# A two-layer hybrid decoder on one core: eight more weight units split into two fp32r parts, and the splitting done in instructions of 1024 columns

## The chip, the cores and the metric

One NeuronCore of one Trainium2 chip runs the kernel; nothing else runs on the core. The metric is the time of one execution in microseconds of device time, taken from runs on the chip. Besides the runs there is one execution recorded by the hardware profiler. Its records are what every row below is read from. Engines are named as the profile names them: PE is TensorE (matrix multiply), PEld its weight loads, DVE is VectorE, ACT is ScalarE, POOL is GpSimd, SP is the engine that issues the large DMAs.

## What is computed

256 tokens of 1024 channels pass through two layers in fp32. Cut to what matters:

```python
def reference(x, ...):
    for layer in range(2):
        h = rmsnorm(x, mix_norm[layer])
        if layer == 0:                       # conformer conv (512 ch) beside attention (8 heads x 64)
            u = h @ ab_w_in                  # 1024 x 2560
            ya = silu(layernorm(conv31(u_val * sigmoid(u_gate))))
            yb = causal_attention_with_alibi(q, k, v)
            y = concat([ya, yb]) @ ab_w_out  # 1024 x 1024
        else:                                # Griffin recurrent block
            gate, xr = split(h @ c_w_in)     # 1024 x 2048
            xr = conv4(xr) + conv_b
            y = (rg_lru(xr) * gelu(gate)) @ c_w_out   # 1024 x 1024
        x = x + y
        x = x + square(relu(rmsnorm(x, mlp_norm[layer]) @ w_up[layer])) @ w_down[layer]   # 1024 x 4096 x 1024
    return rmsnorm(x, final_norm)
```

The weights are about 96 MB in all and are read once.

## The kernel before

**Units and pieces.** Activations are kept transposed, channels on the 128 partitions and 256 tokens along the free dimension. Weights arrive in *pieces* of 1 MB (two DMAs of 512 KB, issued by SP), and each piece is two *units* of 128 x 1024 numbers. A unit is either 128 columns of a projection over all 8 blocks of input channels (kind "c", function `cols`) or 128 rows of a projection with all 1024 output columns (kind "r", function `rows`).

**Three places.** `piece` gives every piece a place. A "raw" piece lies in one of five raw buffers and is multiplied as fp32. A "pair" piece is loaded straight into one of eight pairs of buffers (`wh`, `wl`) and is multiplied as fp32 too; here the two buffers just hold the two units. A "split" piece lands in a raw buffer, and each of its units is then split into a high part `wh` (the number rounded to fp32r) and a low part `wl` (the rest), which takes one of the eight pairs for one unit. A split unit is multiplied with three fp32r matmuls instead of one fp32 matmul: `wh` with the high part of the activation, `wh` with its low part, `wl` with its high part (function `mm`). For that the activation is split as well (`split_act`: a `move` for the high part, a subtraction for the low part). An fp32 matmul shows in the trace as two instructions on `bank_a<-arena,wh` or `bank_a<-arena,wl` when a "pair" unit is used.

**Splitting a unit.** `weights` does it in two halves of 512 columns: a `move`, which either ACT (line 397) or DVE (line 398) may execute, writes half of `wh`; a DVE subtraction (line 312) writes that half of `wl`. 148 units are split this way, so there are 296 moves and 296 subtractions.

**Which units are split.** All of both MLPs (`w_up`, `w_down`), the 16 units of `c_w_in`, and four of the eight units of `ab_w_out`, those fed by the attention heads. The other four units of `ab_w_out` (fed by the conformer branch, after `ln`) and all eight of `c_w_out` (fed by the recurrent block) are "pair" units, multiplied as fp32.

**Around the projections.** `ln` in layer 0 computes mean and variance over channels with matmuls against a tile of ones, scales, and applies Silu on ACT; its results are `mx[0..3]`. `out_cols` then runs the four fp32 units of `ab_w_out`, output block by output block, and `residual_chunk` adds each pair of blocks to the residual and splits it for the MLP. In layer 1, `xr_tail` does the width-4 convolution on DVE (one tensor_scalar and three scalar_tensor_tensor), `gates` the two gate matmuls, `recur_a` an Exp, a Tanh and a square `a2`, `recur_b` a Sqrt, `recur_c` the scan, and `gate_out` the Gelu and the product `mx[c]`; `out_rows` uses `mx[0..3]` with the first four units of `c_w_out`, `out_cols` uses `mx[4..7]` with the last four.

**The order of the work.** Nothing is written in the order in which it runs. Every instruction is added to a `Plan` with an estimated cost per engine and its dependencies; `schedule` runs a list scheduler forward and backward ten times, keeps the shortest result, and `emit` issues each engine's instructions in that order. Each engine executes its own queue strictly in order, so an instruction that waits holds back everything behind it on that engine. The planner takes the DMAs in program order with a rate of 360 KB per us; parts carry a lift in rank (`weights` -2, `ln` +2).

Of the kernel before, what the change touches and what calls it, by code (L numbers as in the profile page):

```python
# [11 lines left out]
P = 128  # L12
S = 256
# [315 lines left out]
def hybrid_trunk(ctx, tc, x, mix_norm, mlp_norm, w_up, w_down, ab_w_in, ab_conv_w, ab_ln_g, ab_ln_b,  # L329
# [111 lines left out]
    def dma(out, in_, size):  # L441
        return plan.add("S", [("dma_start", (out, in_), {})], [out], [in_], {"S": 0.0}, size=size)
# [3 lines left out]
    ones = tl("ones", (P, P))  # L446
# [9 lines left out]
    shared = {t.tensor.name: f"{n}{i}" for n, ts_ in (("wh", whs), ("wl", wls)) for i, t in enumerate(ts_)}  # L456
    plan.shared = {n: 0 for n in shared}

    def renew(name, form):
        return sb.tile([P, KD * P], F32R if form % 2 else F32, name=f"{shared[name]}_{form}", tag=shared[name])  # L460
# [54 lines left out]

    def piece(kind, ap, place):
        n = len(pieces)
        pieces.append((kind, ap))
        us = [len(units), len(units) + 1]
        units.extend([(n, 0), (n, 1)])  # L520
        if place == "pair":
            i = turn["pair"] % NSPL
            turn["pair"] += 1
            homes.append((whs[i], wls[i]))
        else:
            raw = raws[turn["raw"] % NRAW]
            turn["raw"] += 1
            homes.append((raw[:, :1024], raw[:, 1024:]))
        if place == "split":
            for u in us:  # L530
                pairs[u] = turn["pair"] % NSPL
                turn["pair"] += 1
        return us
# [5 lines left out]
    def rows(ap, place):  # L539
        return piece("r", ap, place)  # L540
# [4 lines left out]
    def load(n, lo=0, hi=KD):  # L545

        taken[1] = n + 1
        kind, ap = pieces[n]
        for j, home in enumerate(homes[n]):
            if home.tensor.name in shared:  # L550
                take(home, 0)
            if kind == "ri":
                dma(home.rearrange("p (k c) -> p k c", k=KD), (c_w_r, c_w_i)[j][0].rearrange("h i j -> i h j"), P * 4096)
                continue
            if kind == "gv":
                dma(home.rearrange("p (k c) -> p k c", k=KD)[:, lo:hi], ap[j][:, lo:hi], P * 512 * (hi - lo))
                continue
            h = ap.shape[1] // 2
            a, b = (j * h, j * h + h) if kind == "r" else (max(lo, j * h), min(hi, j * h + h))
            if a < b:  # L560
                dst = home.rearrange("p (a b) -> p a b", a=h)
                dma(dst[:, a - j * h:b - j * h], ap[:, a:b], P * 4096 * (b - a) // h)

    @plan.part
    def weights(u):

        while taken[0] <= u:
            v = taken[0]
            n, j = units[v]
            taken[0] += 1  # L570
            while taken[1] <= n:
                load(taken[1])
            home = homes[n]
            if pieces[n][0] == "c":
                src = [home[k // 4].rearrange("p (k c) -> p k c", k=4)[:, k % 4, j * P:(j + 1) * P] for k in range(KD)]
                half = [home[h].rearrange("p (k c) -> p k c", k=4)[:, :, j * P:(j + 1) * P] for h in range(2)]
            else:
                t = home[j].rearrange("p (k c) -> p k c", k=KD)
                src = [t[:, k] for k in range(KD)]
                half = [t[:, :4], t[:, 4:]]  # L580
            if v not in pairs:
                got[v] = src
                continue
            wh, wl = (t[pairs[v]] for t in (whs, wls))
            take(wh, 1)
            take(wl, 1)
            wh, wl = (t.rearrange("p (k c) -> p k c", k=KD).bitcast(F32R) for t in (wh, wl))
            for h in range(2):
                q = slice(4 * h, 4 * h + 4)
                move(wh[:, q], half[h])  # L590
                tt(wl[:, q], half[h], wh[:, q].bitcast(F32), OP.subtract)
            got[v] = (wh, wl)
        return got[u]
# [15 lines left out]
    for k in (4, 6, 0, 2):  # L609
        u_o[k], u_o[k + 1] = rows(wo[:, k:k + 2], "split" if k > 3 else "pair")  # L610
# [21 lines left out]
    for k in range(0, 8, 2):  # L632
        u_co += rows(wco[:, k:k + 2], "pair")
    u_up[1], u_dn[1] = mlp_units(1)

# [13 lines left out]
    memset(ones, 1.0, "V")  # L649
    memset(eps_t, EPS, "V")  # L650
# [56 lines left out]

    def split_act(src, scale, tag, bufs, engs="V"):
        t = rot(tag, bufs, (P, 2 * S), F32R)
# [8 lines left out]

    def scaled(src, scale):
        t = rot("xg", KD)  # L720
        move(t, src, scale)
        return t
# [23 lines left out]
    def x_chunk(k):  # L746
        b = bank("a")
        transposes([(b[:, t * P:(t + 1) * P], xrow[k * XP // KD][:, t, k % (KD // XP) * P:(k % (KD // XP) + 1) * P], ident) for t in range(2)])
        xs[k] = scaled(b[:, :S], par("mix", k))
# [179 lines left out]
    def ln():  # L929
# [3 lines left out]
        mms([(b[:, :S], ones, mean, True, False)])  # L933
        mms([(b[:, :S], ones, y[3], False, True)])
        act(mean, b[:, :S], AF.Copy, scale=1.0 / 512)
        sq = [ssum, rot("nsq", 2), sumb, rot("nsq", 2)]
        for c in range(4):
            tt(y[c], y[c], mean, OP.subtract)
# [8 lines left out]
        for c in range(4):  # L947
            tt(y[c], y[c], mean, OP.mult)
            act(y[c], y[c], AF.Silu, scale=par("lng", c), bias=par("lnb", c))
            mx[c] = y[c]  # L950
# [148 lines left out]
    def xr_tail(c, b):  # L1099
# [3 lines left out]
        ts(t, xp[:, 0:S], par("cw", c), par("cb", c), OP.mult, OP.add)  # L1103
# [15 lines left out]
    def recur_a(c):  # L1119
# [5 lines left out]
        tt(a2, a, a, OP.mult)  # L1125
# [19 lines left out]
    def gate_out(c):  # L1145
        act(ym[c], ym[c], AF.Gelu_apprx_tanh)
        tt(gi[c], ym[c], xc[c], OP.mult)
        mx[c] = gi[c]
# [115 lines left out]
```

## Time and profile before

| | |
|---|---|
| median of 3 runs | 568.79 us (568.79 to 569.5) |
| the profiled execution, its own time | 569.07 us |
| its span, first to last instruction | 567.3 us |
| PE busy | 558.9 us, 2985 matmul instructions |
| PEld busy | 482.2 us |
| DVE busy | 415.4 us, 962 instructions |
| ACT busy | 310.9 us, 641 instructions |
| POOL busy | 7.5 us |
| mean granted TensorE clock | 0.998 of 2.4 GHz |
| DMA | 98.71 MB, mean 174 GB/s |

The profiled execution's own time is its span and 1.8 us around it. The end of a matmul is modelled by the profiler and matmuls overlap, so the busy time of PE is read together with the start of the next matmul: the distance between starts is what a matmul costs the queue. A group's mean duration is the time of one instruction by itself; a run of n instructions on one line of the timeline shows what they take back to back.

### The profile page before, as it was taken

Reading aid. Unit: us, or ns where it says so; the run is one execution under the profiler, and the core shown is the slowest. Engines: PE = TensorE matmul, PEld = TensorE weight load, DVE = VectorE, ACT = ScalarE, POOL = GpSimd, SP = SyncE. Lnnn points to the kernel's source line nnn. Section 1 sums busy time; section 2 is a strip of 40 time slices with the busy share of each in tenths; the row PEclk is TensorE's granted clock in tenths of the full one; section 3 lists DMA queues with packets and bytes.
Section 4 is the critical chain, followed back from the end, with each engine's and each line's share of the span. In section 5 each row is a group of like instructions: output and inputs, shape, how many; then the busy total and the mean of one; then the engine's idle time right before and its main releaser. Section 6 shows DMA issues by size and latency. Waiting matters only on the chain.

```text
span 567.3 us, 8519 instructions
## 1 busy us (share of the span) xinstructions
PE 558.9 (99%) x2985; PEld 482.2 (85%) x2985; DVE 415.4 (73%) x962; ACT 310.9 (55%) x641; POOL 7.5 (1%) x31
## 2 busy tenths in 40 slices
PE   8999999999999999999999999999999999999995
PEld 7887849988888888888889999888888888888884
DVE  2899998889766765776649999869677667757722
ACT  5104134667655656565537797728555655565623
POOL 5000000000000000000000000000000000000000
PEclk9999999999999999999999999999999999999999
DMA  8991493316666566565009738945656665662001
GB/s 241 283 375 73 138 323 134 122 56 193 196 209 192 172 200 197 175 197 174 0 1 278 242 123 280 370 157 156 199 167 191 210 192 172 202 203 93 1 1 75
DMA packets 71739, 98.71 MB, mean 174 GB/s; under 512 B 3368, under 2 KB 59776, under 8 KB 71696
## 3 DMA queue, kind: packets, MB, share of 16 engines
q1 hardware_dynamic: 71408, 98.06, 55.0%
q8 instruction: 23, 0.38, 0.3%
q14 instruction: 20, 0.16, 0.1%
q0 software_dynamic: 288, 0.11, 0.1%
HBM read 97.11 MB, written 1.05 MB: 173 GB/s over the span
## 4 chain that ended last, share of the span: by engine, by line
PE 94%; DMA 3%; DVE 2%; issue 1%; SPq 0%; ACT 0%; DVEq 0%; ACTq 0%
PE bank_b L312 50%; PE bank_a L312 44%; DMA raw<-in_ab_w_out_dram 2%; DVE arena L312 1%; DMA arena<-in_x_dram 1%; DVE wl L312 0%; SPq L312 0%; ACT arena L312 0%; ACT wh L397 0%; DVE xg L398 0%; DVE x L398 0%; DVE x L312 0%; DVE xT L398 0%; ACT tiny L312 0%; DVE tiny L312 0%
## 5 line engine op out<-in xcount | busy, mean ns | idle before, releaser
L312 DVE TENSOR_TENSOR wl<-raw,wh 128x512 fp32r<-128x512 f32 x296 | 197.0, 687 | 97.5 <-PE bank_b L312 75.6
L397 ACT ACTIVATE wh<-raw 128x512 fp32r<-128x512 f32 x265 | 163.8, 629 | 114.7 <-PE bank_a L312 53.7
L312 PE MATMUL bank_b<-x,wh 128*128 128x512 f32 (+1 forms) x768 | 169.7, 356 | 0.0
L312 PE MATMUL bank_a<-wh,f 128*128 128x512 f32 x512 | 158.5, 391 | 0.0
L312 PEld LDWEIGHTS bank_b<-x,wh 128*128 128x128 f32 x768 | 136.3, 189 | 20.3
L312 PEld LDWEIGHTS bank_a<-wh,f 128*128 128x128 f32 x512 | 94.2, 188 | 18.1
L312 PE MATMUL bank_b<-x,wl 128*128 128x256 f32 x640 | 102.6, 283 | 0.0
L312 PE MATMUL bank_a<-wl,f 128*128 128x512 f32 x256 | 99.6, 389 | 0.0
L312 PEld LDWEIGHTS bank_b<-x,wl 128*128 128x128 f32 x640 | 90.2, 191 | 2.5
L312 PEld LDWEIGHTS bank_a<-wl,f 128*128 128x128 f32 x256 | 48.1, 188 | 10.2
L312 DVE SCALAR_TENSOR_TENSOR arena<-arena,wcol 128x256 f32<-128x256 f32 x120 | 50.7, 484 | 0.2
L312 ACT ACTIVATE relu<-bank_b 128x256 f32<-128x256 f32 x64 | 24.5, 383 | 32.0 <-PE bank_b L312 30.4
L312 PE MATMUL bank_b<-xg,raw 128*128 128x256 f32 x160 | 35.8, 380 | 0.0
L312 PEld LDWEIGHTS bank_b<-xg,raw 128*128 128x128 f32 x160 | 29.9, 190 | 3.9
L312 ACT ACTIVATE relu<-relu 128x256 f32<-128x256 f32 x64 | 23.7, 410 | 17.1 <-DVE relu L312 17.0
L312 DVE TENSOR_TENSOR relu<-bank_b,relu 128x256 f32<-128x256 f32 x64 | 26.6, 419 | 3.9 <-ACT relu L312 3.9
L312 ACT ACTIVATE arena<-arena 128x256 f32<-128x256 f32 (+2 forms) x39 | 18.8, 522 | 16.2 <-DVE arena L312 15.6
L312 PE MATMUL bank_a<-arena,wl 128*128 128x256 f32 x96 | 26.3, 379 | 0.0
L312 PE MATMUL bank_a<-arena,wh 128*128 128x256 f32 x96 | 26.3, 379 | 0.0
L312 DVE TENSOR_TENSOR f<-relu,f 128x256 fp32r<-128x256 f32 x64 | 25.3, 419 | 0.5 <-ACT f L397 0.5
L312 DVE SCALAR_TENSOR_TENSOR relu<-relu,rstd 128x256 f32<-128x256 f32 x64 | 24.4, 419 | 0.1
L312 DVE TENSOR_TENSOR xT<-bank_a,xT 128x256 f32<-128x256 f32 x24 | 8.9, 419 | 15.8 <-PE bank_a L312 15.8
(127 smaller groups left out, 443.6 us busy)
## 6 DMA issues: line engine op xcount, KB each, us to landing
raw<-in_w_up_dram SPq DMA_DIRECT2D x64, 512.0 KB, 4.5
raw<-in_w_down_dram SPq DMA_DIRECT2D x64, 512.0 KB, 4.3
raw<-in_c_w_in_dram SPq DMA_DIRECT2D x16, 512.0 KB, 7.0
raw<-in_ab_w_in_dram SPq DMA_DIRECT2D x8, 512.0 KB, 8.1
wh<-in_ab_w_in_dram SPq DMA_DIRECT2D x5, 512.0 KB, 9.2
wl<-in_ab_w_in_dram SPq DMA_DIRECT2D x5, 512.0 KB, 9.6
raw<-in_ab_w_out_dram SPq DMA_DIRECT2D x4, 512.0 KB, 10.5
wh<-in_c_w_out_dram SPq DMA_DIRECT2D x4, 512.0 KB, 3.4
```

The costliest lines, as they stand in the source:

```text
L312: r.append(getattr(self.engines[o.eng], method)(*map(sub, a), **{n: sub(v) for n, v in k.items()}))
L397: return e.activation(sub(out), sub(a), AF.Copy, **({"scale": scale} if ap else {}))
```

## The change

It does these things. (1) The last four units of `ab_w_out` and the first four of `c_w_out` become "split" units; `mx[0..3]` in both layers is split by `split_act` into four tiles `xg` of twice the old width (two tiles each of the old eight make one). (2) All split units but the first four of each `w_up` and the eight of `ab_w_out` are split in one `move` and one subtraction of 1024 columns instead of two each of 512. (3) Two instructions per channel block of the recurrent layer go from DVE to ACT: the first tap of the convolution (tensor_scalar to Identity with scale and bias) and the square `a2`. (4) In `ln` the mean is taken with a tile holding 1/512, so that the copy that scaled it on ACT falls away and the subtraction reads PSUM. (5) The planner multiplies the estimated size of each DMA by a factor that depends on the length of its contiguous lines.

```diff
-    def dma(out, in_, size):
+    def dma(out, in_, size, line=4096):
+
+        size *= {512: 1.24, 1024: 1.02, 2048: 0.95}.get(line, 0.9)
         return plan.add("S", [("dma_start", (out, in_), {})], [out], [in_], {"S": 0.0}, size=size)
...
+    xgs = [tl(f"xg{i}", (P, 2 * S)) for i in range(4)]
...
             home = homes[n]
             if pieces[n][0] == "c":
...
-                half = [home[h].rearrange("p (k c) -> p k c", k=4)[:, :, j * P:(j + 1) * P] for h in range(2)]
...
-            for h in range(2):
-                q = slice(4 * h, 4 * h + 4)
-                move(wh[:, q], half[h])
-                tt(wl[:, q], half[h], wh[:, q].bitcast(F32), OP.subtract)
+
+            if pieces[n][0] == "c":
+                raw = raws[rawat[n]].rearrange("p (k c) -> p k c", k=KD)[:, :, j * P:(j + 1) * P]
+            else:
+                raw = t
+            n_ = 1 if v in whole else 2
+            for h in range(n_):
+                q = slice(KD // n_ * h, KD // n_ * (h + 1))
+                move(wh[:, q], raw[:, q])
+                tt(wl[:, q], raw[:, q], wh[:, q].bitcast(F32), OP.subtract)
             got[v] = (wh, wl)
...
-    u_o[k], u_o[k + 1] = rows(wo[:, k:k + 2], "split" if k > 3 else "pair")
+    u_o[k], u_o[k + 1] = rows(wo[:, k:k + 2], "split")
...
-        u_co += rows(wco[:, k:k + 2], "pair")
+        u_co += rows(wco[:, k:k + 2], "split" if k < 4 else "pair")
     u_up[1], u_dn[1] = mlp_units(1)
+    whole.update(u_up[0][4:] + u_dn[0] + u_xr + u_gt + u_co + u_up[1][4:] + u_dn[1])
...
+    memset(ones_c, 1.0 / 512)
...
     def split_act(src, scale, tag, bufs, engs="V"):
-        t = rot(tag, bufs, (P, 2 * S), F32R)
+        if tag == "m":
+            t = xgs[next(turns)]
+            take(t, 1)
+            t = t.bitcast(F32R)
+        else:
+            t = rot(tag, bufs, (P, 2 * S), F32R)
...
         b = bank("b")
-        mms([(b[:, :S], ones, mean, True, False)])
-        mms([(b[:, :S], ones, y[3], False, True)])
-        act(mean, b[:, :S], AF.Copy, scale=1.0 / 512)
+        mms([(b[:, :S], ones_c, mean, True, False)])
+        mms([(b[:, :S], ones_c, y[3], False, True)])
...
-            tt(y[c], y[c], mean, OP.subtract)
+            tt(y[c], y[c], b[:, :S], OP.subtract)
...
             act(y[c], y[c], AF.Silu, scale=par("lng", c), bias=par("lnb", c))
-            mx[c] = y[c]
+            mx[c] = split_act(y[c], None, "m", 4)
...
-        ts(t, xp[:, 0:S], par("cw", c), par("cb", c), OP.mult, OP.add)
+        act(t, xp[:, 0:S], AF.Identity, scale=par("cw", c), bias=par("cb", c))
...
-        tt(a2, a, a, OP.mult)
+        act(a2, a, AF.Square)
...
-        mx[c] = gi[c]
+        mx[c] = split_act(gi[c], None, "m", 4) if c < 4 else gi[c]
```

## Rows read from the trace of the kernel before

**Rows 1.** The profile page, the chain of work that ended last: each engine's share of the span.

```profile
PE 94%; DMA 3%; DVE 2%; issue 1%; SPq 0%; ACT 0%; DVEq 0%; ACTq 0%
```

**Rows 2.** Waits of PE over the whole span: who was waited for, us in total, times, the longest.

```profile
PE bank_a L312 <- DVE eps L312: 1.1, 1, 1.1
PE bank_b L312 <- DVE arena L312: 0.7, 1, 0.7
PE bank_a L312 <- DMA arena<-in_x_dram: 0.4, 1, 0.4
PE bank_b L312 <- ACT arena L312: 0.2, 1, 0.2
```

**Rows 3.** Busy time of the engines by stretch (us from the span's start, the stretch's length, then busy us and number of instructions of PE, PEld, DVE, ACT, POOL, the granted clock, the DMA share, GB/s).

```profile
84.00:97.50 13.50, 13.41 (x99) 12.09 (x99) 11.96 (x54) 6.64 (x22) 0.00 (x0) 1.00 0.45 160
97.50:109.25 11.75, 11.75 (x95) 11.49 (x94) 10.62 (x28) 8.10 (x15) 0.00 (x0) 1.00 0.26 73
109.25:123.00 13.75, 13.75 (x67) 11.83 (x65) 9.69 (x26) 5.30 (x14) 0.00 (x0) 1.00 0.26 92
123.00:301.00 178.00, 178.00 (x912) 152.49 (x911) 121.80 (x254) 106.47 (x217) 0.00 (x0) 1.00 0.51 155
...
296.50:322.20 25.70, 25.49 (x190) 24.11 (x189) 23.70 (x57) 17.96 (x37) 0.00 (x0) 1.00 0.93 286
322.20:355.30 33.10, 33.10 (x260) 32.56 (x261) 31.93 (x78) 29.77 (x56) 0.00 (x0) 1.00 0.54 182
355.30:369.10 13.80, 13.80 (x66) 12.09 (x65) 11.75 (x25) 9.55 (x18) 0.00 (x0) 1.00 1.07 370
```

**Rows 4.** Timeline of PE at the start of `c_w_out`: the first four fp32 units, 16 instructions each, and the start of what follows (start us, us, engine, line, operation, tiles, shape, count).

```profile
355.32 3.62 PE L312 MATMUL bank_a<-arena,wh 128*128 128x256 f32 x16
...
365.69 3.62 PE L312 MATMUL bank_a<-arena,wl 128*128 128x256 f32 x16
369.14 0.60 PE L312 MATMUL bank_a<-arena,wh 128*128 128x256 f32 x2
```

**Rows 5.** Timeline of PE in the split units of `ab_w_out` before: the start of one group of three matmuls, and, sixteen groups later, the start of the first fp32 unit.

```profile
103.50 0.40 PE L312 MATMUL bank_a<-x,wh 128*128 128x256 f32 x2
...
109.25 0.60 PE L312 MATMUL bank_a<-arena,wh 128*128 128x256 f32 x2
```

**Rows 6.** Groups of instructions by line, engine, operation and shape: count, then busy us and mean ns of one, then the idle time before them and its releasers.

```profile
L312 DVE TENSOR_TENSOR wl<-raw,wh 128x512 fp32r<-128x512 f32 x296 | 197.0, 687 | 97.5 <-PE bank_b L312 75.6 <-ACT wh L397 18.0 <-PE bank_a L312 3.6
L397 ACT ACTIVATE wh<-raw 128x512 fp32r<-128x512 f32 x265 | 163.8, 629 | 114.7 <-PE bank_a L312 53.7 <-PE bank_b L312 36.9 <-DMA raw<-in_ab_w_out_dram 9.0
...
L312 DVE TENSOR_TENSOR f<-relu,f 128x256 fp32r<-128x256 f32 x64 | 25.3, 419 | 0.5 <-ACT f L397 0.5
...
L397 ACT ACTIVATE f<-relu 128x256 fp32r<-128x256 f32 x53 | 19.3, 402 | 0.1
L312 ACT ACT_TABLE_LOAD x15 | 19.2, 1283 | 1.8 <-PE bank_b L312 0.9 <-PEq L1250 0.7
...
L312 DVE TENSOR_SCALAR arena<-arena,pcol 128x256 f32<-128x256 f32 x8 | 3.1, 414 | 0.0
...
L312 ACT ACTIVATE arena<-arena 128x1024 f32<-128x1024 f32 x2 | 2.1, 1057 | 0.4 <-issue 0.4
L312 ACT ACTIVATE arena<-arena,pcol 128x256 f32<-128x256 f32 x4 | 2.1, 591 | 0.0
```

**Rows 7.** Timeline of ACT and of DVE just after the recurrence: eight moves and nine subtractions of 512 columns back to back.

```profile
360.02 4.25 ACT L397 ACTIVATE wh<-raw 128x512 fp32r<-128x512 f32 x8
...
361.29 5.50 DVE L312 TENSOR_TENSOR wl<-raw,wh 128x512 fp32r<-128x512 f32 x9
```

**Rows 8.** Timeline around 44 us of ACT, DVE and PE: the first splits of `ab_w_out`, and the wait of PE behind them.

```profile
44.16 0.69 DVE L312 TENSOR_TENSOR wl<-raw,wh 128x512 fp32r<-128x512 f32 x1 [1.32 <-ACT wh L397]
...
45.17 0.42 DVE L312 SCALAR_TENSOR_TENSOR arena<-bank_b,rstd 128x256 f32<-128x256 f32 x1
...
45.73 0.89 PE L312 MATMUL bank_b<-arena 64*128 64x256 f32 x4 [0.71 <-DVE arena L312]
```

**Rows 9.** Timeline of DVE and ACT at the end of `ln`: the reciprocal of the standard deviation, a subtraction of `weights` for the MLP put between, the products, the load of the Silu table, the four Silu, and later subtractions for the MLP.

```profile
104.26 1.75 DVE L312 RECIPROCAL arena<-arena 128x256 f32<-128x256 f32 x1
105.93 0.63 DVE L312 TENSOR_TENSOR wl<-raw,wh 128x512 fp32r<-128x512 f32 x1
106.48 1.42 DVE L312 TENSOR_TENSOR arena<-arena 128x256 f32<-128x256 f32 x4
107.81 1.28 DVE L312 TENSOR_TENSOR wl<-raw,wh 128x512 fp32r<-128x512 f32 x2
...
107.10 1.28 ACT L312 ACT_TABLE_LOAD   x1
108.40 2.08 ACT L312 ACTIVATE arena<-arena,pcol 128x256 f32<-128x256 f32 x4
```

**Rows 10.** Waits of ACT for the DMAs of `c_w_in` (us in total, times, the longest).

```profile
ACT wh L397 <- DMA raw<-in_c_w_in_dram: 4.5, 7, 1.1
```

**Rows 11.** Timeline of SP: the issue of the last two pieces of `ab_w_out`, of the last piece of `c_w_out`, and of the first pieces of the second `w_up`.

```profile
62.14 0.33 SPq L312 DMA_DIRECT2D wh<-in_ab_w_out_dram  x1
...
344.29 0.38 SPq L312 DMA_DIRECT2D wl<-in_c_w_out_dram  x1
...
348.81 5.30 SPq L312 DMA_DIRECT2D raw<-in_w_up_dram  x6
```

More of the change, by code (lines that the diff above doesn't have):

```diff
@@ L439, in small_dma @@
         return plan.add("G", [("dma_start", (out, in_), {})], [out], [in_], {"G": 0.55}, lag=4.0)
-    def dma(out, in_, size):
+    def dma(out, in_, size, line=4096):
+        size *= {512: 1.24, 1024: 1.02, 2048: 0.95}.get(line, 0.9)
         return plan.add("S", [("dma_start", (out, in_), {})], [out], [in_], {"S": 0.0}, size=size)
     ident = tl("ident", (P, P))
-    ones = tl("ones", (P, P))
+    ones, ones_c = tl("ones", (P, P)), tl("ones_c", (P, P))
     pcol = tl("pcol", (P, P))
@@ L455, in hybrid_trunk @@
     wls = [tl(f"wl{i}", (P, KD * P)) for i in range(NSPL)]
-    shared = {t.tensor.name: f"{n}{i}" for n, ts_ in (("wh", whs), ("wl", wls)) for i, t in enumerate(ts_)}
+    xgs = [tl(f"xg{i}", (P, 2 * S)) for i in range(4)]
+    shared = {t.tensor.name: (f"{n}{i}", list(t.shape)) for n, ts_ in (("wh", whs), ("wl", wls), ("xg", xgs))
+              for i, t in enumerate(ts_)}
     plan.shared = {n: 0 for n in shared}
     def renew(name, form):
-        return sb.tile([P, KD * P], F32R if form % 2 else F32, name=f"{shared[name]}_{form}", tag=shared[name])
+        tag, shape = shared[name]
+        return sb.tile(shape, F32R if form % 2 else F32, name=f"{tag}_{form}", tag=tag)
     def take(t, part):
@@ L514, in hybrid_trunk @@
     turn = {"raw": 0, "pair": 0}
+    rawat, whole = {}, set()
     def piece(kind, ap, place):
@@ L526, in piece @@
             raw = raws[turn["raw"] % NRAW]
+            rawat[n] = turn["raw"] % NRAW
             turn["raw"] += 1
@@ L552, in load @@
             if kind == "ri":
-                dma(home.rearrange("p (k c) -> p k c", k=KD), (c_w_r, c_w_i)[j][0].rearrange("h i j -> i h j"), P * 4096)
+                dma(home.rearrange("p (k c) -> p k c", k=KD), (c_w_r, c_w_i)[j][0].rearrange("h i j -> i h j"), P * 4096, 512)
                 continue
             if kind == "gv":
-                dma(home.rearrange("p (k c) -> p k c", k=KD)[:, lo:hi], ap[j][:, lo:hi], P * 512 * (hi - lo))
+                dma(home.rearrange("p (k c) -> p k c", k=KD)[:, lo:hi], ap[j][:, lo:hi], P * 512 * (hi - lo), 512)
                 continue
@@ L561, in load @@
                 dst = home.rearrange("p (a b) -> p a b", a=h)
-                dma(dst[:, a - j * h:b - j * h], ap[:, a:b], P * 4096 * (b - a) // h)
+                dma(dst[:, a - j * h:b - j * h], ap[:, a:b], P * 4096 * (b - a) // h, ap.shape[2] * 4)
     @plan.part
@@ L579, in weights @@
                 src = [t[:, k] for k in range(KD)]
-                half = [t[:, :4], t[:, 4:]]
             if v not in pairs:
@@ L706, in narrow @@
             mms([(b[:, :S], w[1][:, j, :], xs[j][0], False, j == KD - 1) for j in range(k, k + 4)])
+    turns = (i % len(xgs) for i in range(1000))
     def split_act(src, scale, tag, bufs, engs="V"):
-        t = rot(tag, bufs, (P, 2 * S), F32R)
+        if tag == "m":
[4 more added lines that the diff above has]
+            t = rot(tag, bufs, (P, 2 * S), F32R)
         h, lo = t[:, :S], t[:, S:]
@@ L717, in split_act @@
         return h, lo, t
[L719 to L722, printed above, removed]
     def residual_chunk(k, acc, gname, g0, xs):
@@ L748, in x_chunk @@
         transposes([(b[:, t * P:(t + 1) * P], xrow[k * XP // KD][:, t, k % (KD // XP) * P:(k % (KD // XP) + 1) * P], ident) for t in range(2)])
-        xs[k] = scaled(b[:, :S], par("mix", k))
+        xs[k] = xgs[k // 2][:, k % 2 * S:(k % 2 + 1) * S]
+        move(xs[k], b[:, :S], par("mix", k))
         move(xT[k], b[:, :S])
```

## The prediction

> **What bounds the kernel now.** I read the chain of waits first: the reader should see there that 94% of the span is PE [rows 1], so time is won mainly by asking less of PE. Then the waits of PE: inside the run it stands still for 0.7 us behind DVE and 0.2 us behind ACT, and the other two entries are the start-up [rows 2]. So there is next to no idle time of PE to win back; a change of DVE or ACT alone can win about 0.9 us. Third, the table by stretch, for the cover under PE. In the first MLP DVE is busy 121.80 of 178 us and ACT 106.47, a third of slack. In the recurrent block, 296.5 to 355.3, DVE is busy 23.70 + 31.93 = 55.63 of 58.8 us and ACT 17.96 + 29.77 = 47.73: 3.2 and 11.1 us free, 14.2 together. There PE is fed just in time [rows 3].
>
> **The eight units, on PE.** Before, four fp32 units take 369.14 - 355.32 = 13.82 us, 3.455 us each [rows 4]. Split, a unit is eight groups of three matmuls; sixteen such groups run from 103.50 to 109.25, which makes 5.75 / 2 = 2.875 us a unit [rows 5]. The gain is 0.58 us a unit, 8 x 0.58 = **4.64 us**. The split groups are of exactly this shape (256 columns, fp32r), so this size is measured, not guessed, and PE has no other work beside it that would hide it.
>
> **What the eight units cost elsewhere.** Each needs a move of `wh` and a subtraction of `wl`. The four of `ab_w_out` go in halves: on DVE 8 x 0.687 = 5.5 us by the mean of one, 8 x 0.61 = 4.9 back to back (5.50 us for nine) [rows 6, 7]; on ACT 8 x 0.53 to 0.63 = 4.2 to 5.0. Those of `c_w_out` go whole. Splitting `mx` adds a move of 0.40 and a subtraction of 0.42 us for each of eight chunks [rows 6], on a path that ends at PE.
>
> *Layer 0.* The four units and `mx[0..3]` must be ready when `out_cols` begins, at 109.25 before. Silu starts at 108.40 and four take 2.08 [rows 9], so `mx[0]` is ready within 0.3 us of its use: the path through `ln` is just in time, and the split of `mx` puts about 0.40 + 0.42 and two hand-overs, some 1.1 us, behind it. Against that, the copy of the mean on ACT goes (about 0.4 us), and the planner has 0.63 us of MLP subtraction standing between the reciprocal and the products which it can move away. DVE has to fit 4.9 to 5.5 us of `wl` and 1.7 of `mx` before about 110; it is free for 13.5 - 11.96 + 11.75 - 10.62 = 2.7 us from 84 on, and the MLP's subtractions now done there (three in rows 9, more after 109) can wait. Net I take a stall of **0.5 us**; bounds 0 (all fits into the gaps) and 2.5 (1.1 of latency, and 6.6 less 2.7 less 2.5 of work that finds no place). What was pushed back must be done by the start of the MLP: the stretch from 109.25 shrinks by 2.3 us, DVE has 13.75 - 9.69 = 4.1 free in it [rows 3]; four units in halves want 5.5, but the second pair is needed only one pass of PE later, so I add nothing and keep 1 us for the range.
>
> *Layer 1.* `out_rows` needs one unit and one `mx` each 2.9 us from about 355 on, and DVE has 2 us free in the 13.8 after that, ACT 4.2 [rows 3]. For the whole block to 355 I count pessimistically, with all four units in it. ACT: eight Identity by the row of the same form (two per-partition operands), 8 x 0.59 = 4.7; eight squares by the nearest 256-column row, 8 x 0.40 = 3.2; four moves of 1024, by the 1024-column row at most 1.06 each, 4.2; four moves of `mx`, 1.6. DVE loses 8 x 0.414 and 8 x 0.42 = 6.7 and gains four subtractions, 0.61 + 512 x (0.687 - 0.419) / 256 = 1.15 each, 4.6, and 1.7 for `mx`. With the gain of the wide instructions below, ACT +12.1 and DVE -1.6: 10.5 us more for 14.2 us of slack, of which the moves may go to either engine. It fits, barely; I take a stall of **0.5 us**, bounds 0 and 2.5 (three chunks of added hand-over of 0.8).
>
> **Wide instructions.** A move of 1024 columns bounds from above at 1.06 us (a 1024-column ACT row that also accumulates), two of 512 are 1.26 by their means [rows 6]: 0.2 us a unit. But the row of eight back to back says 4.25 / 8 = 0.53 us each [rows 7], so two cost 1.06 and one of 1024, at 0.53 + 0.43, about 0.96: 0.1 us a unit. For DVE likewise 1.22 against 1.15, 0.07 us, where the means would give 0.15. I take the back-to-back values, since the moves mostly stand in runs. For the 140 wide units it is 14 us of ACT and 10 of DVE, nearly all under PE in the MLPs: worth **0**. A wide pair hands over later: the low part is complete after 0.96 + 1.15 us instead of 0.53 + 2 x 0.61, some 0.36 us later; eight buffer pairs, two passes ahead, cover that in the MLPs. If that cover were gone (a unit split only as it is used), 0.36 us for each of 140, 50 us, is the outer end, and no row shows PE waiting for `wh` or `wl` in the MLPs, so I give it no weight.
>
> **DMAs and queues.** Eight 512 KB transfers change their buffer. The last two pieces of `ab_w_out`, issued from 62.14 on when their pairs came free, go to raw buffers which are free by about 40; they come earlier, and the pieces behind them on SP too. The first two pieces of `c_w_out` go to raw buffers; the last two wait for later projections, so the `w_up` pieces behind them on SP (first at 348.81 [rows 11]) slip by some 3 us, and are used only past 380: nothing. POOL gets one more memset at the start, nothing waits for it.
>
> **The planner's rates.** ACT and then DVE wait for the first `ab_w_out` piece at 44 us because the plan had it there earlier; DVE loses 1.32 us and PE 0.71 [rows 8]. With lines of 512 bytes counted 1.24 times, the plan expects it later. Of the 0.7 us I take **0.3**; bounds -0.7 and +0.7, as the new order may put another wait there.
>
> **The sum.** 569.07 (the profiled execution: a span of 567.3 and 1.8 around it) - 4.64 + 0.5 + 0.5 - 0.3 = 565.1. The median of the runs is 0.28 lower than that execution, so **564.8 us**.
>
> **Rivals.**
>
> *Late hand-overs.* The two stalls lie nearer their upper ends, 1 to 2 us each and the 0.7 us at 44 stays: 569.07 - 4.64 + 2 to 4 - 0.28, 566.2 to 568.2, 567 in the middle. For it: Silu starting at 108.40 for a use at 109.25, and DVE at 32 of 33 us. Against: the small steps of DVE around 88 to 98 belong to layer 1 and can wait.
>
> *ACT becomes the bound in the recurrent block.* If the planner leaves the moves on ACT, 12.1 us more meet 11.1 us of slack, of which 4.5 us is waiting for DMAs of `c_w_in` [rows 10] in strict order, with Identity, which the convolution now needs, queued behind it; and a changed order can add table loads at 1.28 us [rows 6]. The block then ends 12.1 - 11.1 + 4.5 + 2 x 1.28 = 8.1 us later: 569.07 - 4.64 + 8.1 - 0.28 = 572.3, slower. It decides once the block's lateness passes 4.6 us. Against: DVE has 1.6 us less to do in the block than before, so the planner has somewhere to put moves. The rows show a first tap at 0.414 us on DVE and at 0.59 on ACT, a square at about 0.42 and 0.40 [rows 6]. The Trainium skill, page "ScalarE: Activation LUTs", section "Rules for kernel authors", says that multiplies and adds belong on VectorE and not on ScalarE, which speaks against part (3) of the change. By that rule the block would lose the eight differences of the taps if all of them lay on the path, 8 x 0.18 = 1.4 us, and the sum would be 566.2; the trace of before bears the rule out for the tap, not for the square.
>
> *The change doesn't free PE.* If the order shifts elsewhere by as much as the units give (a start of the MLP held up, a wait at the start), the time stays: 568.5. Only the fitting planner could do it; no row names the place.
>
> *More than the sum.* No stall, and the whole 0.9 us of waits gone: 569.07 - 4.64 - 0.9 - 0.28 = 563.2; lower it can hardly go, since PE's work then has no gap left but start and end.
>
> **Chances.** Forecast (563.4 to 566.3) 0.60; late hand-overs (566.3 to 568.2) 0.20; ACT the bound 0.12; no gain 0.04; more than the sum 0.04. The range 563.2 to 568.3 leaves out the ACT case, part of the last two, under 0.2. What a measurement tells from no change is about 0.2%, 1.1 us, so faster is below 567.65: 0.60 + 0.04 + 0.16 of the late hand-overs = 0.80. Within 0.2%: 0.04 of these, 0.04 of no gain and 0.01 of the ACT case, 0.09. Slower: 0.11.
>
> **What would show it.** The fp32 matmuls on `bank_a<-arena,wh` and `,wl` should fall from 96 each to 32, and new fp32r groups of `bank_a` with `xg` start every 0.36 us; moves and subtractions of 1024 should count 140 and take about 1.06 and 1.22 us alone, those of 512 32. The time from the first `ab_w_out` unit to the MLP should fall by 2.3 us and the `c_w_out` stretch too. It would be wrong if PE showed waits of over 1 us for ACT or DVE around 109 or between 310 and 367, if ACT shows more than 15 table loads, or if the MLP passes of PE became longer.

## The result and the profile after

The changed kernel takes 565.69 us (median of 4 runs, 565.48 to 566.32), the kernel before 569.1 beside it (568.79 to 569.5). The ratio is 0.9944, 95% interval 0.9928 to 0.9959: 3.4 us faster, where 4.0 were forecast. The profiled execution took 565.66 us, with a span of 563.9. Of all executions below, two slow ones are left out of the figures, one of 801.6 us at a mean granted clock of 0.65 and one of 1133.18 us.

The page after: the chain that ended last.

```profile
PE 90%; DVE 4%; DMA 3%; ACT 2%; issue 1%; SPq 1%; ACTq 0%; DVEq 0%
```

PE is still the bound, but its share of the chain fell from 94 to 90% [rows 1], and DVE's and ACT's grew. From 299.73 to 339.51 us this chain now runs through the DMAs, ACT and DVE, up to a wait of PE. The waits of PE after (us, times, the longest):

```profile
PE bank_a L312 <- DVE eps L312: 1.1, 1, 1.1
PE bank_b L312 <- DVE wl L312: 0.9, 1, 0.9
PE bank_a L312 <- DMA arena<-in_x_dram: 0.9, 2, 0.7
PE bank_b L312 <- DVE arena L312: 0.2, 1, 0.2
```

Beside [rows 2]: the 0.7 us behind DVE inside the run went, and a new one of 0.9 us behind a `wl` came. The groups of instructions that answer to [rows 6] (count, busy us and mean ns, idle before them):

```profile
L312 DVE TENSOR_TENSOR wl<-raw,wh 128x1024 fp32r<-128x1024 f32 x140 | 170.4, 1221 | 88.9 <-PE bank_b L312 61.1 <-ACT wh L397 25.7 <-issue 2.2
L397 ACT ACTIVATE wh<-raw 128x1024 fp32r<-128x1024 f32 x108 | 113.7, 1058 | 98.1 <-PE bank_a L312 48.9 <-PE bank_b L312 47.4 <-DMA raw<-in_c_w_in_dram 1.6
...
L398 DVE CAST wh<-raw 128x1024 fp32r<-128x1024 f32 x32 | 22.1, 690 | 0.2 <-PE bank_a L312 0.2
...
L312 ACT ACT_TABLE_LOAD x13 | 16.7, 1283 | 0.9 <-PEq L1267 0.7
...
L312 PE MATMUL bank_a<-arena,wh 128*128 128x256 f32 x32 | 9.5, 378 | 0.0
...
L312 ACT ACTIVATE arena<-arena,pcol 128x256 f32<-128x256 f32 x12 | 6.7, 596 | 2.1 <-DVE arena L312 2.1
```

The fp32 matmuls on `arena` fell to 32 with `wh` and as many with `wl`, and the moves of 1024 columns count 108 + 32 = 140, as do the subtractions. To see where the 3.4 us lie, the long pieces of the chain in order of time are set against each other (start us, length, engine and tile, instructions). The kernel before:

```profile
16.09 17.09 PE bank_b L312 x80
...
123.31 17.14 PE bank_b L312 x98
...
283.54 17.24 PE bank_a L312 x80
...
355.48 27.68 PE bank_a L312 x128
383.16 17.15 PE bank_b L312 x98
...
545.13 16.36 PE bank_a L312 x72
```

The kernel after:

```profile
16.29 52.94 PE bank_b L312 x246
...
120.70 17.13 PE bank_b L312 x98
...
280.92 17.29 PE bank_a L312 x80
...
353.92 25.38 PE bank_a L312 x160
379.30 17.15 PE bank_b L312 x98
...
541.28 16.36 PE bank_a L312 x72
```

The distances between starts give the stages: start-up 16.09 and 16.29 (+0.2); layer 0 up to the first MLP 107.22 and 104.41 (-2.8); first MLP without its last 17 us 160.23 and 160.22; these 17 us and the recurrent block, up to `c_w_out`, 71.94 and 73.00 (+1.1); `c_w_out` 27.68 and 25.38 (-2.3); second MLP 161.97 and 161.98; from the last long piece to the end of the span 22.17 and 22.62 (+0.45). The sum is -3.4, the difference of the spans.

So `c_w_out` gave what its units should, layer 0 fell by 2.8 (what of that is the units' comes below), the MLPs don't get shorter or longer by the wide instructions, and the recurrent block gave back 1.1. Its timeline shows how. ACT after (the last column is the idle time before, and who ended it):

```profile
312.37 1.06 ACT L397 ACTIVATE wh<-raw 128x1024 fp32r<-128x1024 f32 x1 [1.41 <-DMA raw<-in_c_w_in_dram]
...
314.32 2.13 ACT L397 ACTIVATE wh<-raw 128x1024 fp32r<-128x1024 f32 x2
316.47 1.28 ACT L312 ACT_TABLE_LOAD   x1
317.76 1.57 ACT L312 ACTIVATE arena<-bank_b,arena 128x256 f32<-128x256 f32 x4
319.20 0.61 ACT L312 ACTIVATE arena<-arena,pcol 128x256 f32<-128x256 f32 x1
```

DVE in the same stretch, and later:

```profile
313.95 2.16 DVE L312 SCALAR_TENSOR_TENSOR arena<-arena,pcol 128x256 f32<-128x256 f32 x5 [0.45 <-ACT arena L312]
...
319.85 0.49 DVE L312 SCALAR_TENSOR_TENSOR arena<-arena,pcol 128x256 f32<-128x256 f32 x1 [1.68 <-ACT arena L312]
...
338.23 2.37 DVE L312 TENSOR_TENSOR wl<-raw,wh 128x1024 fp32r<-128x1024 f32 x2
```

And PE:

```profile
339.51 0.39 PE L312 MATMUL bank_b<-x,wl 128*128 128x256 f32 x1 [0.91 <-DVE wl L312]
```

The `arena<-arena,pcol` on ACT at 319.20 is a first tap of the convolution, moved there by part (3). It stands behind two moves, a table load and four other activations, and all of these behind a move that waited 1.41 us for a DMA of `c_w_in` (312.37). DVE, which has the other taps to add, waits 1.68 us for this tap, and 0.45 for an earlier one. From there on DVE is busy without a gap up to 338.23, where it is late with the `wl` that PE needs. In that stretch it also executes three moves of 0.69 us (at 324.04, 327.96 and 337.29) that the planner gave to it and not to ACT.

### The profile page after: what moved, and what is told of

The parts are those of the page before. It is cut to its first block, busy times and chain, and to the rows that moved or that the text cites. A ratio compares the mean times of both kernels' runs of the same rounds, so it can differ in the third digit from the quotient of the medians.

```text
span 563.9 us, 8295 instructions
## 1 busy us (share of the span) xinstructions
PE 554.5 (98%) x3049; PEld 481.3 (85%) x3049; DVE 426.5 (76%) x857; ACT 278.4 (49%) x511; POOL 7.7 (1%) x32
## 3 DMA queue, kind: packets, MB, share of 16 engines
HBM read 97.11 MB, written 1.05 MB: 174 GB/s over the span
## 4 chain that ended last, share of the span: by engine, by line
PE 90%; DVE 4%; DMA 3%; ACT 2%; issue 1%; SPq 1%; ACTq 0%; DVEq 0%
PE bank_b L312 47%; PE bank_a L312 43%; DVE arena L312 2%; DMA raw<-in_c_w_in_dram 2%; DVE wl L312 2%; DMA arena<-in_x_dram 1%; ACT arena L312 1%; SPq L312 1%; ACT wh L397 1%; ACT L312 0%; DVE wh L398 0%; ACT nsq L312 0%; DVE xT L312 0%; DVE ssum L312 0%; ACT x L397 0%
## 5 line engine op out<-in xcount | busy, mean ns | idle before, releaser
L312 DVE TENSOR_TENSOR wl<-raw,wh 128x1024 fp32r<-128x1024 f32 (+1 forms) x172 | 190.8, 1123 | 88.9 <-PE bank_b L312 61.1
L397 ACT ACTIVATE wh<-raw 128x1024 fp32r<-128x1024 f32 (+1 forms) x138 | 131.3, 964 | 129.3 <-PE bank_b L312 59.5
L312 ACT ACTIVATE arena<-arena 128x256 f32<-128x256 f32 (+2 forms) x47 | 20.9, 502 | 16.4 <-DVE arena L312 15.8
L312 PE MATMUL bank_a<-xg,wh 128*128 128x256 f32 x128 | 23.1, 283 | 0.0
L398 DVE CAST wh<-raw 128x1024 fp32r<-128x1024 f32 (+1 forms) x34 | 22.9, 674 | 0.2 <-PE bank_a L312 0.2
L312 PEld LDWEIGHTS bank_a<-xg,wh 128*128 128x128 f32 x128 | 20.0, 192 | 0.0
```

The costliest lines, as they stand in the source:

```text
L312: r.append(getattr(self.engines[o.eng], method)(*map(sub, a), **{n: sub(v) for n, v in k.items()}))
L397: return e.activation(sub(out), sub(a), AF.Copy, **({"scale": scale} if ap else {}))
L398: return e.tensor_scalar(sub(out), sub(a), scale, None, op0=OP.mult) if ap else e.tensor_copy(sub(out), sub(a))
```

## The experiments

Three questions were open. Is the gain really the units, or the plan that came with them? Is the lost time of the recurrent block due to the tap on ACT, or to the wide splits, which hand over later? And what are the planner's line factors worth, which I had at 0.3 us? The time of the kernel before beside these runs was 568.6 to 568.83 us (medians of 13). Every edit also made the planner find another order, so a run shows what an edit and its order are worth together. In the edits, `...` stands between places of the program.

**The units alone**: everything else of the change undone, apart from the edit of `ln`.

```diff
-        size *= {512: 1.24, 1024: 1.02, 2048: 0.95}.get(line, 0.9)
...
-    whole.update(u_up[0][4:] + u_dn[0] + u_xr + u_gt + u_co + u_up[1][4:] + u_dn[1])
...
-        act(t, xp[:, 0:S], AF.Identity, scale=par("cw", c), bias=par("cb", c))
+        ts(t, xp[:, 0:S], par("cw", c), par("cb", c), OP.mult, OP.add)
...
-        act(a2, a, AF.Square)
+        tt(a2, a, a, OP.mult)
```

> The eight units split and the edit of ln alone: all units split in halves of 512, first tap and square on DVE, the planner's DMA sizes as before. If the units are the gain, PE loses 4.64 us of matmul time and the run comes out 2 to 4.5 us under the kernel before, 564.6 to 567.1. If the wide instructions, the moved instructions and the line factors are worth nothing or were needed for cover, the difference to the whole change shows it: 565.7 if they were worth nothing; 567 or more, with PE waits of over 2 us for DVE between 300 and 367, if the relief of DVE was needed to carry the extra splitting.

Measured: 568.11 us (10 runs, 567.28 to 568.89), ratio 0.9989 (0.9980 to 0.9999). The units by themselves bring only 0.6 us. Its timeline of PE has the largest wait:

```profile
365.59 0.38 PE L312 MATMUL bank_a<-xg,wl 128*128 128x256 f32 x1 [1.71 <-DVE wl L312]
```

and 19 table loads stand in its trace, four of them between 356.58 and 362.30. The hand-over in layer 1, which I had at 0.5, is 1.7 us in this plan. Which of the parts left out it takes to shorten it, this run doesn't show.

**The first tap back on DVE**, all else as changed.

```diff
-        act(t, xp[:, 0:S], AF.Identity, scale=par("cw", c), bias=par("cb", c))
+        ts(t, xp[:, 0:S], par("cw", c), par("cb", c), OP.mult, OP.add)
```

> The change with the first tap back on DVE (tensor_scalar), all else kept. Theory tap: DVE stood 1.68 and 0.45 us behind Identity on ACT between 313 and 320, and that lateness is the 0.9 us that PE waits for wl at 339.5; then that wait goes and the run is about 0.9 us shorter, 564.8. Theory wide: the wait comes from one subtraction of 1024 columns handing over late; then it stays, 565.7, or grows by the 8 x 0.41 us that DVE gets back, up to 567.

Measured: 564.2 us (4 runs, 563.78 to 564.36), ratio 0.9922 (0.9908 to 0.9937). This is the fastest kernel of the study; it beats the kernel before by 4.5 us and the changed one by 1.2 (by the ratios to the kernel before) to 1.5 us (by the medians). The interval of its ratio overlaps a little with that of the changed kernel, but its runs do not meet those of the next experiment on the same chip (565.32 to 565.74), which equals the changed kernel in time. Its chain:

```profile
281.02 17.29 PE bank_a L312 x80
...
353.05 25.38 PE bank_a L312 x160
378.42 17.15 PE bank_b L312 x98
...
540.40 16.36 PE bank_a L312 x72
```

The stage to `c_w_out` is 353.05 - 281.02 = 72.03, against 71.94 before the change and 73.00 with it, and PE waits for a `wl` only 0.2 us. So the tap on ACT, with the order that it gives, is the lost microsecond of the block. That it goes through the 1.68 us that DVE waited is argued from the chain and not isolated: with the tap on DVE, DVE stands behind ACT for 3.2 us in three waits and PE hardly notices. None of the moves of the block are on DVE in this run. The last long piece starts 545.13 - 540.40 = 4.7 us earlier than before. That this is so near the 4.64 of the units is partly luck, since the old wait of 0.7 is in it too, and 0.3 of start-up and 0.3 in layer 0 and the block against it. ACT has 15 table loads here and 13 in the changed kernel, so their number alone does not make the difference.

**The units of `c_w_out` and `c_w_in` split in halves again**, the MLPs' in one.

```diff
-    whole.update(u_up[0][4:] + u_dn[0] + u_xr + u_gt + u_co + u_up[1][4:] + u_dn[1])
+    whole.update(u_up[0][4:] + u_dn[0] + u_up[1][4:] + u_dn[1])
```

> The change with the units of c_w_in and c_w_out split in halves again; the MLPs stay wide. Theory wide: PE's wait of 0.9 us for wl at 339.5 falls to 0.3 or less, since a half comes 0.6 us earlier, and the run is 0.5 to 0.9 us shorter, 564.8 to 565.2. Theory tap: DVE has about 1.2 us more to do and the wait stays or grows, 565.7 to 566.9.

Measured: 565.66 us (565.32 to 565.74), ratio 0.9948 (0.9931 to 0.9964): the same as the changed kernel. The wait for the `wl` falls from 0.9 to 0.5 us. From the first MLP to `c_w_out` the trace is 0.7 us shorter (120.98 to 353.48, against 120.70 to 353.92); 0.3 us more were lost ahead of it, so PE's last long piece starts 0.4 us earlier than in the changed kernel (541.28):

```profile
540.84 16.36 PE bank_a L312 x72
```

The time doesn't show it, since what follows in this trace is 0.4 us longer, 563.9 - 540.84 = 23.1 us in place of 22.6, and nothing that was edited lies there. So the wide pairs have a part in the loss as long as the tap is on ACT, 0.4 us by the wait and 0.7 by the stage. With the tap on DVE the pairs stay wide and the loss goes all the same. It belongs to the two together.

**The planner without the line factors**, all else as changed.

```diff
-        size *= {512: 1.24, 1024: 1.02, 2048: 0.95}.get(line, 0.9)
```

> The change without the factors on the planner's DMA sizes. If these factors removed the PE wait of 0.71 us at 44 us, it is back there and the run is about 0.7 us longer, 566.4; if the wait went because of the new order as a whole, no change within 0.3 us, 565.7.

Measured: 573.79 to 574.24 us in three runs, ratio 1.0095 (1.0078 to 1.0112), slower than before the change. So within the change, as the planner stands, the factors are worth 8 us and not 0.3. The same kernel a second time, for its trace:

> The same kernel as the run without the factors on the planner's DMA sizes, for a profile at full clock: its first profile was taken while the granted clock was 0.65. The time should be 574 again. The profile has to show where 8 us come from. Theory DMA order in time: the plan has weights of c_w_in earlier than they land, puts their splits ahead of other work on ACT or DVE, and PE waits sum to about 8 us between 295 and 355. Theory attention: the same with ab_w_out and the waits lie between 40 and 110.

Measured: 573.48 us (2 runs, 573.02 and 573.95), ratio 1.0086 (1.0065 to 1.0106). Its timeline of PE and then of ACT:

```profile
345.18 0.80 PE L312 MATMUL bank_b<-x,wh 128*128 128x256 f32 x2 [5.26 <-ACT wh L397]
```

```profile
330.46 1.06 ACT L397 ACTIVATE wh<-raw 128x1024 fp32r<-128x1024 f32 x1
331.54 1.28 ACT L312 ACT_TABLE_LOAD   x1
332.83 0.42 ACT L312 ACTIVATE arena<-arena 128x256 f32<-128x256 f32 x1
333.27 1.28 ACT L312 ACT_TABLE_LOAD   x1
334.56 0.84 ACT L312 ACTIVATE arena<-bank_b,arena 128x256 f32<-128x256 f32 x2
335.42 1.28 ACT L312 ACT_TABLE_LOAD   x1
...
340.25 1.28 ACT L312 ACT_TABLE_LOAD   x1
341.55 0.72 ACT L312 ACTIVATE arena<-arena 128x256 f32<-128x256 f32 x2
342.29 1.28 ACT L312 ACT_TABLE_LOAD   x1
343.58 0.60 ACT L312 ACTIVATE arena<-arena 128x256 f32<-128x256 f32 x1
344.09 1.04 ACT L397 ACTIVATE wh<-raw 128x1024 fp32r<-128x1024 f32 x1
```

In 12 us ACT loads a table six times (7.7 us; one is in the lines left out), going back and forth between Sqrt (`arena<-arena`) and, for the most part, the Tanh of the gates (`arena<-bank_b`); the split that PE wants stands behind, at 344.09. The planner did not mean this: its `switch` counts no load for a Tanh as soon as any table is loaded. The stage to `c_w_out` takes 361.68 - 281.54 = 80.1 us, against 73.0. Behind the wait the granted clock falls to its lower level (stretch, length, then busy us and instructions of PE, PEld, DVE, ACT, POOL, granted clock, DMA share, GB/s):

```profile
345.18:348.74 3.56, 3.10 (x12) 2.80 (x13) 3.56 (x7) 3.56 (x8) 0.00 (x0) 0.50 0.02 5
```

**The line factors alone, in the kernel before.**

```diff
-    def dma(out, in_, size):
+    def dma(out, in_, size, line=4096):
+        size *= {512: 1.24, 1024: 1.02, 2048: 0.95}.get(line, 0.9)
... (and the line length passed in the calls)
```

> The kernel before with the factors on the planner's DMA sizes and nothing else. If the factors make the plan better by themselves, the PE wait of 0.71 us at 44 us goes, and the run is 0.5 to 1 us shorter, 567.8. If the 8 us of the run without them are an accident of one plan, it stays within 1.5 us of the kernel before, either way, 567.2 to 570.2. If they are worth 8 us wherever they are, 561.

Measured: 567.26 us (10 runs, 567.1 to 567.76), ratio 0.9978 (0.9968 to 0.9987). Alone they bring 1.3 us: the wait of 0.71 us at 45.73 goes, as expected, and the first MLP starts 123.31 - 121.85 = 1.5 us earlier, so the new order gains about as much again elsewhere in layer 0.

**No wide instructions at all**: the line `whole.update(...)` taken out.

> The change with every unit split in halves of 512. By the prediction the wide instructions are worth nothing: 565.7, within 0.5. Theory cover: in the recurrent block DVE has 20 x 0.07 and ACT 20 x 0.10 us more to do, and PE waits grow by 1 to 3 us, 566.7 to 568.7.

Measured: 565.68 us (565.57 to 566.2), ratio 0.9951 (0.9934 to 0.9967). With 560 instructions of 512 columns in the place of 280 wide ones, the time is the same to 0.01 us: the wide ones are worth nothing in it, as forecast. In the trace that is two differences which cancel: without them PE's last long piece starts 541.28 - 540.81 = 0.5 us earlier, and what follows is 0.5 us longer.

**Tap and square both back on DVE.**

```diff
-        act(t, xp[:, 0:S], AF.Identity, scale=par("cw", c), bias=par("cb", c))
+        ts(t, xp[:, 0:S], par("cw", c), par("cb", c), OP.mult, OP.add)
...
-        act(a2, a, AF.Square)
+        tt(a2, a, a, OP.mult)
```

> The change with both moved instructions, the first tap and the square, back on DVE. Theory tap: the tap on ACT is the whole loss in the recurrent block, the square is indifferent: 564.2, as with the tap alone on DVE. Theory relief needed: with 3.4 us more of squares DVE is late again, PE waits 0.5 to 2 us between 335 and 367, 564.7 to 566.2.

Measured: 565.93 to 566.4 us in three runs, ratio 0.9956 (0.9939 to 0.9973). Part (3) as a whole therefore nets 0.3 to 0.7 us, inside the intervals, but its two halves pull apart. Against the kernel with the tap alone on DVE, the square on ACT is worth 1.8 to 2 us together with the order that it gives: without it, PE waits 0.96 us for DVE at the start of the second MLP (at 382.60), and ACT has 19 table loads in place of 15. How much of the 1.8 the loads are is not shown.

This run also bears on the first experiment. Tap and square are on DVE in both, and the units alone took 568.11 us: 2.1 us of what they lacked came back with the line factors and the wide instructions, that is, with another order, and not with the relief of DVE.

**No line factors, but the planner counts a load for Tanh after Sqrt.**

```diff
-        size *= {512: 1.24, 1024: 1.02, 2048: 0.95}.get(line, 0.9)
...
-        return s is not None and s != self.table and not (o.func == AF.Tanh and self.table)
+        return s is not None and s != self.table and not (o.func == AF.Tanh and self.table not in (None, "sqrt"))
```

> The change without the line factors, and with the planner told that a Tanh after a Sqrt needs a table load (it took Tanh as free in every set). Theory unplanned loads: the run without line factors had 16 loads where its plan counted 12, and the four loads, 5.1 us, are the 5.3 us that PE waited for wh, with some 2 us of half clock behind; counted, they go: no PE wait over 1.5 us, about 565.7, at most 567. Theory DMA times: the plan has the weights too early without the factors, that is not mended, 571 to 574.

Measured: 565.9 us (565.49 to 566.0), ratio 0.9945 (0.9928 to 0.9962), with 14 table loads in place of 16 and no wait of PE over 0.6 us between start-up and end. The 8 us came from the loads that the planner took as free: counting them brings the time back without the line factors. These had only led the plan past that trap by another order, and with the loads counted they are worth nothing here (565.9 against 565.69 us).

**Four more units**: the last four of `c_w_out` split too, `mx[4..7]` in tiles of the MLP; tap on DVE.

```diff
-        u_co += rows(wco[:, k:k + 2], "split" if k < 4 else "pair")
+        u_co += rows(wco[:, k:k + 2], "split")
... (the first tap as above)
-        mx[c] = split_act(gi[c], None, "m", 4) if c < 4 else gi[c]
+        mx[c] = split_act(gi[c], None, "m" if c < 4 else "f", 4 if c < 4 else LAG + 3)
```

> The change with the first tap on DVE, and the last four units of c_w_out split too; mx[4..7] take four tiles of the MLP's f. By the units alone PE loses another 4 x 0.58 = 2.3 us: 561.9, if DVE and ACT carry 4 x (1.15 + 0.96) and 4 x (0.42 + 0.40) us more behind 355. Theory late hand-overs: out_cols waits for the splits or for the last mx, and the run stays at 563.5 to 565.

Measured: 565.7 us (565.01 to 566.17), ratio 0.9943 (0.9928 to 0.9958), 1.5 us over the kernel with the tap alone on DVE, though PE has 4 x 0.58 = 2.3 us less to do. The waits of PE, and the table by stretch around them (stretch, length, then busy us and instructions of PE, PEld, DVE, ACT, POOL, granted clock, DMA share, GB/s):

```profile
366.08 0.39 PE L312 MATMUL bank_a<-f,wl 128*128 128x256 f32 x1 [0.81 <-DVE wl L312]
...
367.55 0.39 PE L312 MATMUL bank_a<-f,wl 128*128 128x256 f32 x1 [0.85 <-DVE wl L312]
```

```profile
367.50:369.00 1.50, 1.45 (x9) 1.46 (x10) 1.50 (x3) 0.00 (x0) 0.00 (x0) 0.77 0.87 309
369.00:371.00 2.00, 2.00 (x12) 2.00 (x11) 2.00 (x3) 0.00 (x0) 0.00 (x0) 0.50 0.88 277
371.00:373.00 2.00, 2.00 (x16) 2.00 (x16) 2.00 (x4) 0.00 (x0) 0.00 (x0) 0.82 1.00 338
```

Two waits of 0.8 us, and then 5.5 us at a granted clock of 0.77, 0.50 and 0.82, which cost, by an estimate from these shares, 1.5 x 0.23 + 2 x 0.5 + 2 x 0.18 = 1.7 us more. Together 3.4 us for a gain of 2.3: from the last 17 us of the first MLP to the start of the second it takes 98.7 us, with four units fewer 97.4.

The same with the Tanh counted, for another order:

> The same with the planner counting the load of a Tanh after a Sqrt. If the unplanned load (15 real, 14 planned) costs something, up to 1.3 us shorter, 560.6 to 561.9; if one such load is hidden by slack, the same within 0.5 us; another plan may also be worse by as much as the plans so far differ in the block, 1 to 2 us, 563.5.

Measured: 565.38 us, from 564.59 to 566.41, ratio 0.9939 (0.9924 to 0.9955). The profile has one wait of 1.2 us for the split of `mx`, and a clock of 1.00 after it. The two lower runs had a mean granted clock of 0.997, the two higher ones 0.993 and 0.994. So in these two orders the last four units bring nothing over the version with the tap on DVE.

**The eight units fp32 again**, with wide splits, square on ACT, line factors, `ln`; tap on DVE, Tanh counted.

```diff
-        u_o[k], u_o[k + 1] = rows(wo[:, k:k + 2], "split")
+        u_o[k], u_o[k + 1] = rows(wo[:, k:k + 2], "split" if k > 3 else "pair")
...
-        u_co += rows(wco[:, k:k + 2], "split" if k < 4 else "pair")
+        u_co += rows(wco[:, k:k + 2], "pair")
...
-            mx[c] = split_act(y[c], None, "m", 4)
+            mx[c] = y[c]
...
-        mx[c] = split_act(gi[c], None, "m", 4) if c < 4 else gi[c]
+        mx[c] = gi[c]
... (the first tap and the count of Tanh as above)
```

> The change with the eight units and their activations back to fp32, with the tap on DVE and the Tanh load counted; wide instructions, the square on ACT, the line factors and the edit of ln stay. If the units are the gain, PE has 4.64 us more: 568.2 to 568.8, against 564.2 of the run with the tap on DVE. If the rest carries part of the gain, less: 566 to 567.5.

Measured: 568.65 us (10 runs, 568.34 to 569.59), ratio 0.9996 (0.9987 to 1.0006): the gain is gone. A group of instructions, then the chain:

```profile
L312 PE MATMUL bank_a<-arena,wh 128*128 128x256 f32 x96 | 26.2, 379 | 0.1
```

```profile
283.96 17.27 PE bank_a L312 x80
...
356.00 27.68 PE bank_a L312 x128
```

The fp32 matmuls are back at 96, `c_w_out` at 27.68 us. Against the kernel with the tap on DVE the difference is 4.45 us, where 4.64 was worked out (the plans also differ by the count of Tanh). Between the two traces 2.30 us lie in `c_w_out` and 1.81 in layer 0, 4.1 of the 4.64; another 1.1 lie in the start-up, which the edit doesn't touch. The stage to `c_w_out` is 72.04 with fp32 units and 72.03 with split ones: with the tap on DVE, the splitting itself costs PE nothing there.

## Why the prediction came out

- *The eight units, 4.64 us.* Right: `c_w_out` shrank by 2.30 of 2.32, layer 0 by 2.8, which can be read as 2.32 and 0.7 of the old wait less 0.2; undoing the units takes 4.45 back. But that the kernel gets this gain is a matter of the order that goes with it: the units alone gave 0.6 us, and 2.6 us with the line factors and the wide instructions beside them, tap and square still on DVE.
- *The hand-over in layer 0, 0.5.* Against the kernel before it comes out at 2.32 + 0.71 - 2.81 = 0.2 us, and no wait of PE at `out_cols` is listed. But the size depends on the kernel that is set beside it. With the units undone, layer 0 was 1.81 us longer, not 2.32, which makes it 0.5. Against the line factors alone (layer 0 from 16.39 to 121.85, 105.46 us) the changed kernel gains only 1.05 there, which makes it 1.3. All three lie within the bounds of 0 and 2.5; the term itself is not settled.
- *The hand-over in layer 1, 0.5.* This is the term that was mis-sized most: 1.1 us, and its cause was not the one I gave. I had asked whether DVE and ACT have room for the splits and the answer, that it fits, was right: from the end of the first MLP to `c_w_out` ACT rose by 4.1 us (44.69 between 300.78 and 355.48 before, 48.78 between 298.20 and 353.92 after), not by 12.1, and DVE fell by 0.5 (52.85 to 52.38), not by 1.6. The taps brought ACT 4.6 us, as counted, but two table loads fewer took off 2.6, three moves of weights and three of the four of `mx` went to DVE, and three of the four wide subtractions of `c_w_out` came only after the block. What cost PE 0.9 us was the order: the tap on ACT, in strict order behind moves and a table load, together with the wide pairs, without which the wait was 0.5.
- *The rival "ACT becomes the bound in the recurrent block".* Its mechanism was real in parts. An Identity queued on ACT behind a move that waited for `c_w_in` stands in the chain of the changed kernel, in small. Extra table loads made the plan without line factors slow; there it was a move, not an Identity, that PE waited for, and ACT was held up by six loads and not by a want of room. That it took 573.5 us, where the rival had 572.3, is luck. It lay as near as one factor in the planner, so a chance of 0.12 was not too much. A row had spoken against the tap: 0.596 us a tap on ACT after, 0.414 on DVE before [rows 6]. By the difference of the taps alone I had 1.4 us; the tap on DVE gains 1.2 to 1.5, of which 1.0 is in the block and 0.4 in the end of the run, which no edit touches. So the size is near, but what the tap cost was not its own longer time on ACT. The Trainium skill, page "ScalarE: Activation LUTs", section "Rules for kernel authors", puts multiplies and adds on VectorE; the runs agree for the tap (564.2 against 565.69 us) and not for the square, which on ACT gains 1.8 to 2 us.
- *Wide instructions, 0.* Right in the time, and in part by luck, since a loss of 0.5 us up to the last long piece and a shorter end cancel. They cost what the rows gave for one (1.06 and 1.22 us) and took ACT's busy time in the first MLP (123 to 280) from 95.88 to 76.74 us, under PE. The price that I named and gave no weight, the later hand-over, did show, 0.4 us of a wait in the recurrent block, and not in the MLPs where I looked for it.
- *The planner's rates, 0.3.* The wait at 45.73 went as a whole (0.7), and the factors alone are worth 1.3 us in the kernel before. But inside the change the wait also goes without them, once the loads of Tanh are counted. What they did there was to keep the plan away from loads that it doesn't count, which is worth 8 us. This I did not see: I priced the plan's changes by the waits of the old trace only.
- *Not in the sum:* start-up +0.2 and the end +0.45. After the last DVE instruction the span lasts 3.7 us before and 4.2 after; over the profiles at full clock it was 3.7, 4.2 or 4.6 without an edit that touches it. So two traces that are equal up to there can differ by 0.9 us in their span. That the whole came within 0.9 us of the forecast is in part luck: layer 0 was 0.3 better and the rates 0.4, against 0.6 worse in layer 1 and 0.65 outside the sum.

Open remains what sets the three lengths of the end, and how much of a difference of under 1 us between two kernels is their edit and how much another order that the planner happened to find: every edit here gave a new order.

## What to carry to other kernels

First count the work that an edit takes from the engine that is the bound, from rows of the same shape: that term held to 1% in `c_w_out` and to 4% in the time of the whole. Then look at the engines that feed it not by how much room they have but by what stands ahead of each handed-over tile in their strict order; moving a small instruction to the idler engine can make it late. And where a planner orders the work, make it count what the trace shows (here the table load of a Tanh after a Sqrt), or any small edit may lead it into a plan that costs more than the edit can win.

## What the runs showed of the hardware

A wait of PE can cost more than its length. After the wait of 5.26 us the granted clock was 0.50, the lower of its two levels (1.2 GHz), from 345.18 to 348.74, and a group of three fp32r matmuls took 0.64 us in place of 0.36; after two waits of 0.81 and 0.85 us 1.5 us apart it fell too, to 0.50 between 369 and 371. After single waits of 0.9, 1.2 and 1.7 us (the changed kernel, the last plan with four more units, the units alone) it stayed at 1.00.

A Tanh after a Sqrt, and a Sqrt after a Tanh, each stand behind a table load of 1.28 us, and that is the whole price of the switch: the load at 331.54 begins 0.02 us after the instruction before it has ended, and the Sqrt starts at 332.83, 0.01 us after the load. The Trainium skill, page "ScalarE: Activation LUTs", section "What ACT_TABLE_LOAD costs", gives 1283 ns for the load, which the trace shows, and 1380 ns of drain beside it, which it doesn't. The measurement decides; by the page the six loads would have held ACT for 16 us in place of the 12 in which they and ten other instructions ran.
